# Block attention's scores issued for two heads at a time, alternating between two PSUM banks, in a one-core decoder block

## The chip, the cores and the metric

The kernel runs on one core of a Trainium2 chip. The metric is the device time of one execution in microseconds (us), the median over runs. TensorE is called PE in the views (its weight loads PEld), VectorE DVE, ScalarE ACT, GpSimd POOL, and SP issues the DMAs.

## The reference, cut to what matters

One hybrid decoder block for 256 tokens of 1024 features: three mixers in parallel (block attention "MoBA", retention, attention to a memory), a gated merge, and a convolutional GeGLU FFN. The change touches only the scores of the block attention, which has 8 heads of 64 features. With 256 tokens and a block of 256, only the query's own block remains, causally masked:

```python
s_own = (jnp.einsum('bhqd,bhnd->bhqn', q_c, k_own).astype(jnp.float32) * scale
         + table[:, rel_bucket(d_own)])
s_own = jnp.where(d_own >= 0, s_own, NEG_INF)
...
p = jax.nn.softmax(logits, axis=-1).astype(v.dtype)
...
return (jnp.einsum('bhqkn,bhqkne->bhqe', p_sel, v_sel)
        + jnp.einsum('bhqn,bhne->bhqe', p_own, v_own))
```

## The kernel before

Activations lie transposed, features on the 128 partitions and tokens on the free axis. The weights stream through in 150 pieces of [128, 1024]. Each piece is split into a high and a low part (ACT writes `whi` at L141, DVE writes `wlo` at L142), and each float32 product is carried by three passes of float32r matmuls: L183 in `unit` (256 columns each, 24 to a piece) and L170 to L172 in `proj_b` (512 columns). `piece()` issues the split three pieces ahead (`LA = 3`).

All small work is put between the pieces: `at(p, fn, ...)` registers it, and `tick()` runs it behind the matmuls of piece p. Every engine executes in the order of this program, so the place in it decides what is queued behind what.

For the block attention `qa` and `ka` are tiles of [128, 4, 256]: a feature tile f holds two heads, the even head on partitions 0 to 63 and the odd one on 64 to 127. `moba_s(h)` computes the scores of one head: one matmul for the later 128 queries against all 256 keys (L366) and one for the earlier 128 against the first 128 keys (L367, the rest is masked), both into one PSUM bank from `s_ps()` (two banks, `sps`). They are plain float32 matmuls with 64 rows, and the profile shows two weight loads and two matmuls for each. DVE then adds the bias (L369) into a scratch tile and takes two maxima (L372). `moba_e` (ACT, L379) exponentiates, `moba_n` (DVE, L385 and L387) normalises, `moba_t` transposes on PE (L391 to L393, read back by ACT at L394), and `moba_v` multiplies with the values for both heads of a feature tile (L405). Feature tile f starts at piece b = 16 + 3f:

```python
for f in range(4):
    b = 16 + 3 * f
    at(b + 5, moba_v, f)
    ...
    for hh in range(2):
        at(b + hh + 3, moba_t, 2 * f + hh)
        at(b + hh + 2, moba_n, 2 * f + hh)
        at(b + hh + 1, moba_e, 2 * f + hh)
        at(b + hh, moba_s, 2 * f + hh)
```

So the scores of the even head stand behind piece b and those of the odd head behind piece b + 1, with a piece of projection between them. Pieces 16 to 27 are the memory attention's projections; while they run, DVE and ACT also write the normed memory (L215 and L214, behind pieces 16 to 19).

`moba_v` is of use for comparison: its four matmuls go in turns to the output partitions 0 to 63 (even head) and 64 to 127 (odd head).

Of the kernel before, what the change touches and what calls it, by code (L numbers as in the profile page):

```python
"""Hybrid decoder block (MoBA attention + retention + memory cross-attention, gated merge, causal
conv GeGLU FFN) on one NeuronCore.

Layout: activations are kept transposed, [features on partitions, tokens on the free axis], so that
projections chain without transposes; values, the retention gate and the FFN output are
token-major.  Every float32 weight product is carried by float32r passes: an operand is split
exactly into hi (its top 12 significant bits) and lo (the rest), and hi*hi + hi*lo + lo*hi are
accumulated in float32.  With SEQ == MOBA_BLOCK no block lies fully in the past of any query, so
MoBA's selected blocks are masked for every query by the shapes alone and the causal own block
remains; likewise retention's state before the first chunk is zero.  # L10

Order: the weights stream through in pieces of [128, 1024] in the order of their use, and every
engine keeps the order of this program; the steps of the norms and of the mixers are set between the
pieces of later projections (at), so that TensorE always has work and no engine waits for the next.
"""
# [16 lines left out]
P = 128  # L32
D = 1024
# [6 lines left out]

# columns of the packed parameters
G_MEM, G_FFN, CONV_W, CONV_B = 0, 8, 16, 16 + 3 * 2 * NF
NPAR = CONV_B + 2 * NF
# columns of the packed constants
C_ID, C_COS, C_SIN, C_DEC, C_QIN, C_KOUT = 0, 128, 384, 640, 1152, 1664
NCONST = 1668
NREL = 384
NQ = 150      # pieces of the weights
LA = 3        # pieces split ahead of their use
WARM = 16  # L50
PASSES = ((0, 0), (0, 1), (1, 0))   # hi*hi + hi*lo + lo*hi
DEFER = 4     # FFN feature tiles that start from the h not yet normed
LAST = 3      # pieces of w_down that finish one group of outputs after the other


@with_exitstack
def block_kernel(ctx, tc, w, xt, mt, par, cst, onehot, relb, gng, gfin, out):
# [11 lines left out]

# [1 line left out]
    def mm_ps():  # L71
# [40 lines left out]

# [1 line left out]
    works = defaultdict(list)  # L114

    def at(p, fn, *args):
        """Run fn behind piece p."""
        works[p].append((fn, args))
# [4 lines left out]

# [1 line left out]
    raws, pieces = [], []  # L125
    count = {"used": 0}

    def load_ahead(n):
        """Start the loads of the first n pairs of pieces."""
        while len(raws) < min(n, NQ // 2):  # L130
            raws.append(raw8())
            nc.sync.dma_start(raws[-1], w[len(raws) - 1])
# [11 lines left out]
    def piece():  # L144
        """The next [128, 1024] piece of the weights as (hi, lo), with LA more split behind it."""
        while len(pieces) < min(NQ, count["used"] + 1 + LA):
            q = len(pieces)
            load_ahead(q // 2 + 3)
            piece_tiles()
            split_cols(q, 0, 1024)  # L150
        count["used"] += 1
        return pieces[count["used"] - 1]

    def split_to(dst, s, src):
        """dst[:, hi and lo, s] = src."""
        nc.scalar.copy(dst[:, 0, s], src)
        nc.vector.tensor_tensor(out=dst[:, 1, s], in0=src, in1=dst[:, 0, s].bitcast(FT), op=OP.subtract)

# [1 line left out]
    def proj_b(src, evac):  # L160
        """512 features, tokens on partitions."""
        ps = [mm_ps(), mm_ps()]
# [14 lines left out]
    def unit(p, hi, lo, o, step, src, nk):  # L177
        """One feature tile; the lo of the last two k, which comes last, is used last."""
        order = [(k, a, b) for k in range(nk - 2) for a, b in PASSES]
        order += [(k, a, 0) for k in (nk - 2, nk - 1) for a in (0, 1)] + [(k, 0, 1) for k in (nk - 2, nk - 1)]  # L180
        for i, (k, a, b) in enumerate(order):
            wk = (hi, lo)[a][:, o + step * k:o + step * k + P]
            nc.tensor.matmul(p, wk, src[:, b, k], start=(i == 0), stop=(i == len(order) - 1))  # L183

    def proj_a(src, banks=1):
        """256 features, features on partitions: a [128, 256] of a bank each."""
        ps = [mm_ps() for b in range(banks)]
        for f in range(2):
            hi, lo = piece()
            unit(ps[f % banks][:, T * f:T * f + T], hi, lo, 0, P, src, KD)  # L190
            tick()
        return kt(ps[0]) if banks == 1 else [kt(p)[:, f] for f, p in enumerate(ps)]

# [1 line left out]
    def rsqrt(dst, ss, n, scale):  # L195
# [4 lines left out]
    def squares(src, acc, i, scalar):  # L200
        """acc += x^2 of the features of pair i."""
        v = src[:, 2 * i:2 * i + 2]
# [14 lines left out]
    class Norm:  # L217
        """rsqrt(mean + eps) of each token, and src * gain * that, split."""

# [6 lines left out]
        def factor_col(self):  # L226
            """Tokens on partitions."""
            ps = t_ps()
# [4 lines left out]
        def factor_row(self):  # L233
            """As a row on all partitions."""
            ps = t_ps()
# [22 lines left out]

# [1 line left out]
    xs = big8()  # L260
# [27 lines left out]

# [1 line left out]
    mhalf = consts.tile([P, 2], FT, name="mhalf")  # L290
# [9 lines left out]

# [1 line left out]
    xg = act16()  # L302
# [15 lines left out]

# [1 line left out]
    nm = Norm("nm", mr, pr[:, G_MEM:G_MEM + KD], kt(w2()))  # L320
# [3 lines left out]

# [1 line left out]
    hank = mix.tile([P, 8, 384], FT, name="hank")  # L326
# [20 lines left out]

# [1 line left out]
    qa, ka, va = qk_tile(), qk_tile(), v_tile()  # L349
# [12 lines left out]

    def moba_s(h):
        f, pp = h // 2, slice(64 * (h % 2), 64 * (h % 2) + 64)
        sp = s_ps()
        nc.tensor.matmul(sp[:, 0:256], qa[pp, f, 128:256], ka[pp, f, :], start=True, stop=True)  # L366
        nc.tensor.matmul(sp[:, 256:384], qa[pp, f, 0:128], ka[pp, f, 0:128], start=True, stop=True)  # L367
        sb = w2()
        nc.vector.scalar_tensor_tensor(sb[:, :384], sp[:, :384], asc, hank[:, h, ::-1], op0=OP.mult, op1=OP.add)  # L369
        mx = act.tile([P, 2], FT, name="amx", bufs=2)  # L370
        for t, s in halves:
            nc.vector.tensor_reduce(out=mx[:, t:t + 1], in_=sb[:, s], axis=AX.X, op=OP.max, negate=True)  # L372
        mo["p", h] = sb, mx

# [36 lines left out]
    for f in range(4):  # L411
        b = 16 + 3 * f
        at(b + 5, moba_v, f)
        if f % 2 == 1:
            at(b + 6, moba_y, f // 2)
        for hh in range(2):
            at(b + hh + 3, moba_t, 2 * f + hh)
            at(b + hh + 2, moba_n, 2 * f + hh)
            at(b + hh + 1, moba_e, 2 * f + hh)
            at(b + hh, moba_s, 2 * f + hh)  # L420

# [1 line left out]
    qm, km = yt_tile(), yt_tile()  # L423
# [67 lines left out]

# [1 line left out]
    cos, sin = ct[:, C_COS:C_COS + T], ct[:, C_SIN:C_SIN + T]  # L493
# [19 lines left out]
    def ret_k():  # L513
        """Decay of chunk 0's keys to its end, times the factor of their norm (which v lacks)."""
        re["k"] = act.tile([P, 4], FT, name="rk", bufs=1)
        nc.vector.tensor_scalar(re["k"], ct[:, C_KOUT:C_KOUT + 4], nx.col[:, 0:1], None, op0=OP.mult)

    def ret_x():
        """Scores of chunk 1's queries with chunk 0's keys."""
        sp, sd = s_ps(), w2()  # L520
# [65 lines left out]

# [1 line left out]
    x2 = {}  # L588
# [35 lines left out]

# [1 line left out]
    hg = act16()  # L626
# [24 lines left out]

# [1 line left out]
    U0 = 84  # L653
# [44 lines left out]

# [1 line left out]
    groups = [[(0, 512, t_ps()), (512, 1024, t_ps())],  # L700
# [36 lines left out]
    def mean(t, i):  # L737
        """(sum of the squares up to group i) / D + eps."""
        v = act.tile([P, 1], FT, name="osv", bufs=4)
# [34 lines left out]

# [1 line left out]
def _constants():  # L776
# [8 lines left out]
    c[half:, C_COS:C_COS + T] = cos  # L785
    # read by the half that it multiplies: out1 -= x2 sin, out2 += x1 sin
    c[:half, C_SIN:C_SIN + T] = sin
# [5 lines left out]
    for h in range(4):  # L793
        c[:, C_DEC + P * h:C_DEC + P * h + P] = np.where(d >= 0, np.exp(lg[h] * np.maximum(d, 0)), 0.0) * ks
        c[:, C_QIN + P * h:C_QIN + P * h + P] = np.exp(lg[h] * (i + 1.0))[None, :]
        c[:, C_KOUT + h] = np.exp(lg[h] * (P - 1.0 - i)) * ks
    # one-hot of the bucket of distance m - 127
    dist = np.arange(NREL) - 127
# [79 lines left out]
```

## Time and profile before

| | us |
|---|---|
| median of 3 runs | 474.81 |
| lowest and highest run | 474.66 and 476.47 |
| span of the profiled execution, first to last instruction | 474.1 |
| PE busy in that span | 464.7 (98%) |
| DVE busy | 349.5 (74%) |
| ACT busy | 259.0 (55%) |

For the profiled execution only its span is on record, and no time of its own beside it; the median of the runs is about 0.7 us above that span. Matmuls are pipelined: a row's duration reaches from issue to a modelled end, and rows overlap. What a matmul costs is therefore read from the distance between the starts of neighbours, not from its duration.

### The profile page before, as it was taken

The numbers are of one execution on the slowest core, as the hardware profiler recorded it, in microseconds if no ns is written. First come the engines' busy times: TensorE is split into PE (matmuls) and PEld (weight loads), VectorE is DVE, ScalarE is ACT, GpSimd is POOL, SyncE is SP. The second block draws the span as 40 slices with busy tenths as digits, with TensorE's granted clock in tenths as the row PEclk, the third lists the DMA queues.
The fourth block names the chain that finished last, engine by engine and source line by source line (L and its number), as shares of the span: only waits on it lengthen the run. The fifth ranks groups of instructions, "written<-read, shape, count | busy, mean of one in ns | idle before, by whom it ended". The sixth has DMA issues, their size and how long they took to land.

```text
span 474.1 us, 8508 instructions
## 1 busy us (share of the span) xinstructions
PE 464.7 (98%) x3470; PEld 439.0 (93%) x3470; DVE 349.5 (74%) x536; ACT 259.0 (55%) x412; POOL 61.9 (13%) x47
## 2 busy tenths in 40 slices
PE   8999999999999999999999999999999999999994
PEld 6799899879989999999999999999999999888883
DVE  5969798766985558676677888979879899744433
ACT  5747465554455543354445555667768676533323
POOL 3344520001320013312000006000000000000003
PEclk9999999999999999999999999999999999999998
DMA  8989634335254544354464575555554545555102
GB/s 249 402 342 291 266 122 150 145 138 178 91 196 160 178 178 147 121 178 178 178 191 166 182 274 211 203 195 196 202 179 162 199 177 179 184 182 197 59 1 88
DMA packets 16342, 86.75 MB, mean 183 GB/s; under 512 B 1672, under 2 KB 4272, under 8 KB 6832
## 3 DMA queue, kind: packets, MB, share of 16 engines
q1 hardware_dynamic: 16016, 85.70, 50.8%
q8 instruction: 27, 0.44, 0.4%
q10 hardware_dynamic: 288, 0.52, 0.3%
q14 instruction: 11, 0.09, 0.1%
HBM read 85.15 MB, written 1.06 MB: 182 GB/s over the span
## 4 chain that ended last, share of the span: by engine, by line
PE 95%; DMA 1%; DVE 1%; ACT 1%; POOL 0%; SPq 0%; issue 0%; POOLq 0%; ACTq 0%
PE mm L183 67%; PE mm L172 3%; PE mm L170 3%; PE mm L171 3%; PE tps L706 2%; PE tps L707 2%; PE tps L708 2%; PE sps L706 1%; PE sps L707 1%; PE sps L708 1%; DMA big<-in_xt 1%; PE sps L366 1%; PE yps L405 1%; PE sps L439 1%; DVE wlo L142 1%; PE yps L476 1%
## 5 line engine op out<-in xcount | busy, mean ns | idle before, releaser
L183 PE MATMUL mm<-act,whi 128*128 128x256 f32 x1600 | 292.2, 282 | 0.0
L183 PEld LDWEIGHTS mm<-act,whi 128*128 128x128 f32 x1600 | 248.0, 188 | 1.8 <-issue 1.0
L142 DVE TENSOR_TENSOR wlo<-raw,whi 128x1024 fp32r<-128x1024 f32 (+1 forms) x154 | 195.4, 1273 | 65.3 <-ACT whi L141 65.0
L141 ACT CAST whi<-raw 128x1024 fp32r<-128x1024 f32 (+1 forms) x154 | 157.8, 1027 | 124.9 <-PE mm L183 75.1
L183 PE MATMUL mm<-act,wlo 128*128 128x256 f32 x800 | 215.5, 280 | 0.0
L183 PEld LDWEIGHTS mm<-act,wlo 128*128 128x128 f32 x800 | 150.7, 188 | 0.0
L674 DVE SCALAR_TENSOR_TENSOR w<-mm,pr,w 128x255 f32<-128x255 f32 (+1 forms) x72 | 29.7, 476 | 10.3 <-ACT w L669 10.2
L183 PE MATMUL mm<-yt,whi 128*128 128x256 f32 x192 | 36.6, 282 | 0.0
L183 PEld LDWEIGHTS mm<-yt,whi 128*128 128x128 f32 x192 | 30.4, 188 | 0.0
L170 PE MATMUL mm<-whi,act 128*128 128x512 f32 x64 | 26.7, 418 | 0.6 <-ACT whi L141 0.6
L669 ACT ACTIVATE w<-mm,pr 128x256 f32<-128x256 f32 x36 | 18.4, 561 | 16.3 <-PE mm L183 16.2
L172 PE MATMUL mm<-wlo,act 128*128 128x512 f32 x64 | 26.2, 410 | 1.0 <-DVE wlo L142 1.0
L171 PE MATMUL mm<-whi,act 128*128 128x512 f32 x64 | 26.1, 408 | 0.0
L183 PE MATMUL mm<-yt,wlo 128*128 128x256 f32 x96 | 25.1, 282 | 0.0
L735 POOL TENSOR_TENSOR hN<-hN,gfb 128x512 f32<-128x512 f32 x2 | 2.6, 1281 | 169.8 <-ACT w L731 169.8
L183 PEld LDWEIGHTS mm<-yt,wlo 128*128 128x128 f32 x96 | 18.1, 188 | 0.0
L505 POOL TENSOR_TENSOR qk<-qk,w 128x512 f32<-128x512 f32 x4 | 9.3, 2314 | 65.7 <-DVE w L503 65.7
L706 PE MATMUL tps<-whi,ah 128*128 128x512 f32 x44 | 17.5, 397 | 0.0
L707 PE MATMUL tps<-whi,ah 128*128 128x512 f32 x44 | 17.4, 396 | 0.0
L172 PEld LDWEIGHTS mm<-wlo,act 128*128 128x128 f32 x64 | 12.4, 194 | 5.4 <-DVE wlo L142 2.5
L708 PE MATMUL tps<-wlo,ah 128*128 128x512 f32 x44 | 17.3, 393 | 0.0
L170 PEld LDWEIGHTS mm<-whi,act 128*128 128x128 f32 x64 | 12.5, 195 | 3.9 <-ACT whi L141 0.9
(162 smaller groups left out, 512.8 us busy)
## 6 DMA issues: line engine op xcount, KB each, us to landing
raw<-in_w SPq DMA_DIRECT2D x72, 1024.0 KB, 4.8
raw<-in_w SPq DMA_DIRECT2D x8, 256.0 KB, 5.8
raw<-in_w SPq DMA_DIRECT2D x2, 512.0 KB, 6.3
big<-in_mt SPq DMA_DIRECT2D x1, 1024.0 KB
hank<-rel_d SPq DMA_DIRECT2D x1, 1024.0 KB, 11.8
raw<-in_xt SPq DMA_DIRECT2D x1, 1024.0 KB, 5.0
ct<-in_cst SPq DMA_DIRECT2D x1, 770.0 KB, 4.4
big<-in_xt SPq DMA_DIRECT2D x3, 256.0 KB, 6.0
```

Source lines behind the costliest of these rows:

```text
L141: nc.scalar.copy(hi[:, a:b], r)
L142: nc.vector.tensor_tensor(out=lo[:, a:b], in0=r, in1=hi[:, a:b].bitcast(FT), op=OP.subtract)
L170: nc.tensor.matmul(ps[t], xh, wh, start=(k == 0), stop=False)
L171: nc.tensor.matmul(ps[t], xl, wh, start=False, stop=False)
L172: nc.tensor.matmul(ps[t], xh, wl, start=False, stop=(k == KD - 1))
L183: nc.tensor.matmul(p, wk, src[:, b, k], start=(i == 0), stop=(i == len(order) - 1))
L505: nc.gpsimd.tensor_tensor(out=d, in0=d, in1=tmp, op=OP.add)
L669: nc.scalar.activation(ac[:, i], ps[:, i], AF.Identity, bias=pr[:, CONV_B + c:CONV_B + c + 1], scale=cw(2, c))
L674: nc.vector.scalar_tensor_tensor(ac[:, i, s:], ps[:, i, :T - s], cw(2 - s, c), ac[:, i, s:], op0=OP.mult, op1=OP.add)
L706: nc.tensor.matmul(p, xh, hi[:, a:b], start=(f == 0), stop=False)
L707: nc.tensor.matmul(p, xl, hi[:, a:b], start=False, stop=False)
L708: nc.tensor.matmul(p, xh, lo[:, a:b], start=False, stop=(f == NF - 1))
```

## The change

`moba_s` now takes a feature tile instead of a head. It takes both PSUM banks, issues the 256-key matmuls of the even and the odd head, then the 128-key matmuls of both, and then does the DVE work of the even head and of the odd head. It runs behind piece b; nothing is left behind piece b + 1. The other steps keep their pieces. (The change also empties docstrings and comments, which moves no instruction and no line number ahead of `moba_s`; behind it lines move by 4.)

```diff
-    def moba_s(h):
-        f, pp = h // 2, slice(64 * (h % 2), 64 * (h % 2) + 64)
-        sp = s_ps()
-        nc.tensor.matmul(sp[:, 0:256], qa[pp, f, 128:256], ka[pp, f, :], start=True, stop=True)
-        nc.tensor.matmul(sp[:, 256:384], qa[pp, f, 0:128], ka[pp, f, 0:128], start=True, stop=True)
-        sb = w2()
-        nc.vector.scalar_tensor_tensor(sb[:, :384], sp[:, :384], asc, hank[:, h, ::-1], op0=OP.mult, op1=OP.add)
-        mx = act.tile([P, 2], FT, name="amx", bufs=2)
-        for t, s in halves:
-            nc.vector.tensor_reduce(out=mx[:, t:t + 1], in_=sb[:, s], axis=AX.X, op=OP.max, negate=True)
-        mo["p", h] = sb, mx
+    def moba_s(f):
+        sps = [s_ps(), s_ps()]
+        for q, k, o in ((slice(128, 256), 256, 0), (slice(0, 128), 128, 256)):
+            for hh in range(2):
+                pp = slice(64 * hh, 64 * hh + 64)
+                nc.tensor.matmul(sps[hh][:, o:o + k], qa[pp, f, q], ka[pp, f, :k], start=True, stop=True)
+        for hh in range(2):
+            h, sp, sb = 2 * f + hh, sps[hh], w2()
+            nc.vector.scalar_tensor_tensor(sb[:, :384], sp[:, :384], asc, hank[:, h, ::-1], op0=OP.mult, op1=OP.add)
+            mx = act.tile([P, 2], FT, name="amx", bufs=2)
+            for t, s in halves:
+                nc.vector.tensor_reduce(out=mx[:, t:t + 1], in_=sb[:, s], axis=AX.X, op=OP.max, negate=True)
+            mo["p", h] = sb, mx
...
     for f in range(4):
...
+        at(b, moba_s, f)
         for hh in range(2):
             at(b + hh + 3, moba_t, 2 * f + hh)
             at(b + hh + 2, moba_n, 2 * f + hh)
             at(b + hh + 1, moba_e, 2 * f + hh)
-            at(b + hh, moba_s, 2 * f + hh)
```

What PE has behind piece 16 before, between that piece (weights `whi_580`) and piece 17 (`whi_602`): the scores of head 0 alone, in one bank (`sps_688`).

```order
L183 MATMUL mm_654<-act16_436,whi_580 128x256 x2
L366 MATMUL sps_688<-qk_264,qk_263 128x256
L367 MATMUL sps_688<-qk_264,qk_263 128x128
L183 MATMUL mm_654<-act16_436,whi_602 128x256 x2
L366 MATMUL sps_733<-qk_264,qk_263 128x256
```

(The last row, head 1, stands behind piece 17, 23 more matmuls of L183 later.) And at the same place with the change, `sps_688` for head 0 and `sps_689` for head 1:

```order
L183 MATMUL mm_654<-act16_436,whi_580 128x256 x2
L370 MATMUL sps_688<-qk_264,qk_263 128x256
L370 MATMUL sps_689<-qk_264,qk_263 128x256
L370 MATMUL sps_688<-qk_264,qk_263 128x128
L370 MATMUL sps_689<-qk_264,qk_263 128x128
L183 MATMUL mm_654<-act16_436,whi_602 128x256 x2
```

The two matmuls of head 1 have moved up by one piece, in between those of head 0; behind piece 17 nothing stands between the projections.

What DVE has from the memory's norm of piece 16 (`w_622`) to the split of the first memory queries (L157, `yt`), as a difference; `w_691` and `w_694` are the scratch tile of head 0, `w_699` that of head 1:

```order
 L215 SCALAR_TENSOR_TENSOR act_683<-w_622,pr,act_683 128x256 x2
-L369 SCALAR_TENSOR_TENSOR w_691<-sps,hank 128x384
-L372 TENSOR_REDUCE amx<-w_691 128x1 x2
+L373 SCALAR_TENSOR_TENSOR w_694<-sps,hank 128x384
+L376 TENSOR_REDUCE amx<-w_694 128x1 x2
+L373 SCALAR_TENSOR_TENSOR w_699<-sps,hank 128x384
+L376 TENSOR_REDUCE amx<-w_699 128x1 x2
 L142 TENSOR_TENSOR wlo<-raw,whi 128x1024
 L215 SCALAR_TENSOR_TENSOR act_683<-w_624,pr,act_683 128x256 x2
-L369 SCALAR_TENSOR_TENSOR w_736<-sps,hank 128x384
-L372 TENSOR_REDUCE amx<-w_736 128x1 x2
 L157 TENSOR_TENSOR yt<-mm,yt 128x512
```

Head 1's bias and maxima have moved ahead of one split of weights (L142) and one pair of the memory's norm; what stands ahead of L157 is the same work in sum.

What PE has behind piece 19 before, where the transposes of head 0 (L391 to L393, which read its normalised scratch tile) stand ahead of head 2's scores:

```order
L183 MATMUL mm_743<-act16_436,whi_655 128x256 x2
L391 MATMUL tps_817<-ct_93,w2_691 128x128
L392 MATMUL tps_817<-ct_93,w2_691 128x128
L393 MATMUL tps_817<-ct_93,w2_691 128x128
L366 MATMUL sps_827<-qk_264,qk_263 128x256
L367 MATMUL sps_827<-qk_264,qk_263 128x128
L183 MATMUL mm_837<-act16_683,whi_698 128x256 x2
```

With the change the transposes stay where they were, and the scores of heads 2 and 3 follow them:

```order
L183 MATMUL mm_743<-act16_436,whi_655 128x256 x2
L395 MATMUL tps_817<-ct_93,w2_694 128x128
L396 MATMUL tps_817<-ct_93,w2_694 128x128
L397 MATMUL tps_817<-ct_93,w2_694 128x128
L370 MATMUL sps_827<-qk_264,qk_263 128x256
L370 MATMUL sps_828<-qk_264,qk_263 128x256
L370 MATMUL sps_827<-qk_264,qk_263 128x128
L370 MATMUL sps_828<-qk_264,qk_263 128x128
L183 MATMUL mm_845<-act16_683,whi_706 128x256 x2
```

Only the scores have moved here: PE reaches these transposes with one block of scores less behind it than before.

## Rows read from the trace of the kernel before

**Rows 1.** The page, part 1: busy us (share of the span) xinstructions.

```profile
PE 464.7 (98%) x3470; PEld 439.0 (93%) x3470; DVE 349.5 (74%) x536; ACT 259.0 (55%) x412; POOL 61.9 (13%) x47
```

**Rows 2.** The page, part 4: the chain that ended last, by engine.

```profile
PE 95%; DMA 1%; DVE 1%; ACT 1%; POOL 0%; SPq 0%; issue 0%; POOLq 0%; ACTq 0%
```

**Rows 3.** Stretches A:B: length, busy us of PE, PEld, DVE, ACT, POOL, clock, DMA share, GB/s.

```profile
57.00:101.00 44.00, 44.00 (x298) 38.45 (x297) 33.43 (x66) 26.34 (x61) 4.85 (x3) 1.00 0.37 129
300.00:400.00 100.00, 100.00 (x852) 100.00 (x851) 88.50 (x159) 70.15 (x119) 0.00 (x0) 1.00 0.53 182
```

**Rows 4.** Groups by form, PE: busy us, mean ns | idle before.

```profile
L366 PE MATMUL sps<-qk 64*128 64x256 f32 x16 | 5.6, 428 | 0.0
```

**Rows 5.** Timeline, PE, head 0's scores behind piece 16: start us, us, instruction.

```profile
59.65 0.28 PE L183 MATMUL mm<-act,whi 128*128 128x256 f32 x1
59.87 0.48 PE L366 MATMUL sps<-qk 64*128 64x256 f32 x1
60.19 0.38 PE L366 MATMUL sps<-qk 64*128 64x256 f32 x1
60.40 0.27 PE L367 MATMUL sps<-qk 64*128 64x128 f32 x1
60.51 0.27 PE L367 MATMUL sps<-qk 64*128 64x128 f32 x1
60.71 0.50 PE L183 MATMUL mm<-act,whi 128*128 128x256 f32 x2
61.05 0.28 PE L183 MATMUL mm<-act,wlo 128*128 128x256 f32 x1
```

**Rows 6.** The chain in order of time: an undisturbed run of L183.

```profile
158.52 14.25 PE mm L183 x120
```

**Rows 7.** Timeline, PE, the value products of heads 0 and 1 behind piece 21.

```profile
78.69 0.28 PE L183 MATMUL mm<-act,whi 128*128 128x256 f32 x1
78.89 0.44 PE L405 MATMUL yps<-w,vv 128*64 128x256 f32 x2
79.16 0.50 PE L405 MATMUL yps<-w,vv 128*64 128x256 f32 x4
79.38 0.39 PE L405 MATMUL yps<-w,vv 128*64 128x128 f32 x4
79.70 0.51 PE L183 MATMUL mm<-act,whi 128*128 128x256 f32 x2
80.04 0.28 PE L183 MATMUL mm<-act,wlo 128*128 128x256 f32 x1
```

**Rows 8.** Timeline, PE: transposes with L183 directly behind them, behind piece 28.

```profile
107.18 0.27 PE L393 MATMUL tps<-ct,w 128*128 128x128 f32 x1
107.21 0.48 PE L183 MATMUL mm<-act,whi 128*128 128x256 f32 x2
```

**Rows 9.** Timeline, DVE: bias of heads 0 and 1, one weight split, the normalisations.

```profile
62.45 0.54 DVE L369 SCALAR_TENSOR_TENSOR w<-sps,hank 128x384 f32<-128x384 f32 x1
...
63.56 1.22 DVE L142 TENSOR_TENSOR wlo<-raw,whi 128x1024 fp32r<-128x1024 f32 x1
...
65.48 0.56 DVE L369 SCALAR_TENSOR_TENSOR w<-sps,hank 128x384 f32<-128x384 f32 x1
...
69.32 0.55 DVE L387 TENSOR_SCALAR w<-w,ari 128x256 f32<-128x256 f32 x2
...
71.91 0.55 DVE L387 TENSOR_SCALAR w<-w,ari 128x256 f32<-128x256 f32 x2
```

**Rows 10.** The stretch of DVE from behind piece 16's norm to head 0's normalisation.

```profile
60.62:69.87 9.25, 9.25 (x74) 8.85 (x73) 9.15 (x20) 7.17 (x18) 1.23 (x1) 1.00 0.37 120
```

**Rows 11.** Timeline, PE: first transposes of heads 0 and 1, first wlo of piece 20.

```profile
70.37 0.27 PE L391 MATMUL tps<-ct,w 128*128 128x128 f32 x1
...
71.98 0.28 PE L183 MATMUL mm<-act,wlo 128*128 128x256 f32 x1
...
74.59 0.27 PE L391 MATMUL tps<-ct,w 128*128 128x128 f32 x1
```

## The prediction

> **What bounds the kernel now.** I read the page first, then the stretches, then PE's timeline round the scores. PE is busy for 464.7 of 474.1 us [rows 1], and 95% of the chain that ended last is PE's [rows 2]. In the stretch that holds all scores, 57 to 101 us, PE is busy for all of its 44.00 us, and it is so again from 300 to 400 us, where DVE comes nearest to it with 88.5 of 100 us [rows 3]. The granted clock is 1.00 in both, the upper level of 2.4 GHz. So the place of the change is bounded by PE's own stream, and what the scores take from that stream is time of the kernel, as long as nobody else becomes late. The views show starts of matmuls; I use only distances between starts.
>
> **What one block of scores costs.** Undisturbed L183 runs at 14.25 / 120 = 0.119 us per matmul [rows 6]. From the last L183 of piece 16 at 59.65 to the third L183 of piece 17 at 61.05 is 1.40 us [rows 5]. Without scores that is three steps, 0.36. Head 0's block therefore costs **1.04 us**, and 8 heads 8.3 us. The starts inside say what it consists of. The two passes of 128 columns start 0.11 apart (60.40 and 60.51), and the second pass of 256 columns takes 0.21 (60.19 to 60.40): columns alone make 2 x 0.21 + 2 x 0.11 = 0.64. The other 0.40 is paid once for each block: 0.09 more than a normal step before the first pass (59.65 to 59.87), 0.11 more for the first pass (0.32 instead of 0.21, as its successor's weights are not loaded in time), 0.09 more behind the last pass (60.51 to 60.71 is 0.20, its columns 0.11), and 0.10 more behind the first L183, whose two starts lie 0.50 - 0.28 = 0.22 apart. All 16 instructions of this form [rows 4] are 8 heads' two passes, one such block each.
>
> **What the change does to it.** Before, 8 blocks of 2 matmuls (4 passes) each; after, 4 blocks of 4 matmuls (8 passes). No column is saved. Four times the 0.40 of entering and leaving is saved in any case. Whether the columns of the odd head cost anything is not shown by any block of scores, because no two matmuls on different row halves are neighbours in this trace. The bounds are: full cost, 0.64 per pair, or nothing, if the two halves of the array stream at the same time.
>
> The nearest row is L405, which alternates between two column halves of the array in the same pattern: even head, odd head, even, odd, with 256 columns twice and then 128 columns twice. Its 8 passes start as four couples at 78.89, 79.16, 79.38 and one between that and 79.70; the row at 78.89 holds two passes in 0.44 us, less than the 0.48 of the first score pass alone [rows 5, 7]. From 78.69 to 80.04 the whole takes 1.35, less 0.36 for three L183 steps: **0.99 us for two heads**, although the columns of its 8 passes, at the prices above, are 4 x 0.21 + 4 x 0.11 = 1.28 us. So two half arrays do stream at the same time there. I take the same for two row halves: a pair of heads then costs what one head costs now, 1.04. Nothing in the rows is nearer, and it is the same engine, the same float32 passes and the same order of issue.
>
> By the Trainium skill, "TensorE: Matmul & The Clock Gate", Part 3 (packing small matmuls), matmuls whose operands lie on different row groups run concurrently, with a measured 3.07x for four of them. The same page of the Trainium skill says that matmuls keep strict program order, which speaks against full couples (a rival below). The trace agrees with the concurrency on column halves; no run here shows it for row halves. The Trainium skill, "TensorEngine Tiling (Array Packing)", Gotcha 1, states that different row tiles cannot access one PSUM bank at the same time; the change gives each head a bank, and no run here shows two in one.
>
> **The sum before waits.** Four blocks vanish, behind pieces 17, 20, 23 and 26. The block behind piece 17 stands between two runs of L183 and saves 1.04. The other three stand behind transposes. There L183 would start 0.03 behind L393, and the second of it 0.48 - 0.28 = 0.20 later [rows 8], so nearly the same is left over: I take 4 x 1.04 = **4.18 us** with the unrounded block of 1.045.
>
> **What becomes late.** PE will be 1.04 us earlier when it comes to the transposes of head 0 behind piece 19: 70.37 - 1.04 = 69.33 [rows 11]. They read the tile that DVE normalises at L387, which ends at 69.32 + 0.55 = 69.87 [rows 9]. Can DVE be earlier too? From 60.62 to 69.87 it is busy for 9.15 of 9.25 us [rows 10]: it is working off a backlog, in which head 0's bias starts at 62.45, 1.7 us behind the scores. The change only reorders this backlog (head 1's bias and maxima, about 1.2 us from 65.48, move ahead of the split at 63.56), so the end stays at 69.87. PE then waits 0.54 us, and the first transpose's weights, no longer loaded ahead, cost another 0.1, as behind each block above. I take **0.65 us given back**; bounds are 0 (DVE earlier by as much) and 1.04 (the whole advance).
>
> Queued behind that wait are the scores of heads 2 and 3, which DVE takes at the end of the same backlog, and piece 20. The next such place is safe: head 1's tile is done at 71.91 + 0.55 = 72.46 [rows 9], and PE comes for it at 74.59 - 1.04 + 0.65 = 74.2 [rows 11]. For heads 2 to 7 the road from scores to transposes gets one block, about 1 us, shorter on PE, but DVE's backlog is gone there: over 57 to 101 us it is busy for only 33.43 of 44 us [rows 3].
>
> The rest costs nothing. The weight split at 63.56 ends 1.2 us later, at 66.0, and PE uses its first low part at 71.98 [rows 9, 11], or 0.4 earlier with the change: 5.6 us cover it; without cover the whole 1.2 would fall on PE. Both banks are asked for together, but their readers of the tile before are DVE steps three pieces (over 9 us) back. No DMA is issued at another place; behind 101 us everything simply comes earlier, and PE is fed without a gap [rows 3].
>
> Net: 4.18 - 0.65 = 3.53 us. The span should go from 474.1 to 470.6, and with the same 0.7 us around it the time from 474.81 to **471.3 us**, -0.74%. With no wait it is 470.6; with the weight loads of the two halves taking turns (0.11 more for each of four pairs) 471.7. That is the forecast's own range, 470.5 to 471.7. About 0.5% (2.4 us) is what a measurement of this kernel can tell from no change.
>
> **Rivals.**
>
> *Strict order.* The odd head may start only when both passes ahead of it have started: then its first pass runs beside the even head's second, and one pass of 256 columns per pair stays uncovered, 0.21 us. The gain is 4 x 0.83 = 3.3; PE comes to head 0's transposes at 69.54 and gives back 0.45. Net 2.9, time **471.9**. For it: the odd head's matmul is issued behind both passes of the even one. Against it: L405 has that same order of issue and starts in couples [rows 7]. This rival is the rule of the Trainium skill named above ("TensorE: Matmul & The Clock Gate", Part 3, matmuls in strict order); the trace disagrees with it on column halves.
>
> *Row halves don't stream together.* Only the four times 0.40 remain, 1.6 us; PE comes at 69.97, so no wait. Time **473.2**, which measures as no change: the edit wouldn't do what it is made for. For it: a row half writes all 128 output partitions, so two of them write twice as much per partition as L405 does. Against it: each has a bank of its own.
>
> *Each turn drains the array.* Entering or leaving a 64-row block costs 0.09 of gap and 0.11 of uncovered load [rows 5]. If a turn from one row half to the other did the same, 3 turns in each of 4 pairs add 12 x 0.20 = 2.4 us to a serial pair: 2.4 - 1.6 = 0.8 slower, **475.6**. It is slower than before from 0.13 us per turn, and slower by over 0.5% from (1.6 + 2.4) / 12 = 0.33. For it: a change of shape costs just that. Against it: L405's turns cost nothing visible.
>
> **How the numbers follow.** Forecast 0.68, strict order 0.10, no overlap 0.14, drains 0.05, something unseen 0.03. The likeliest gives 471.3. Forecast and strict order together hold 0.78, just under what a range should, so it reaches to the third case: 470.4 to 473.3. Faster by over 0.5% are the first two (0.77 with a little off), within it the third and most of the fourth (0.18), slower the rest (0.05).
>
> **What would show it.** Right: four blocks of scores instead of eight; in each the 8 passes start as four couples, and from the L183 ahead of them to the third behind them it is again about 1.40 us; behind piece 17 L183 runs on at 0.119; one wait of PE, about half a microsecond, at the transposes behind piece 19, put down to DVE's L391; and PE ahead by about 3.5 us from there to the end. Wrong: eight separate starts in a block (1.4 + 0.64 us long), gaps of 0.2 us between the heads' passes, or PE waits at later transposes or at a low part of the weights, which would say that DVE or ACT could not follow.

## The result and the profile after

The changed kernel takes **471.81 us** (median of 4 runs, 471.54 to 472.01), against 474.99 for the kernel before (4 runs, 474.66 to 476.47). The ratio is **0.9932, interval 0.992 to 0.9944**: faster by 3.2 us, with an interval of 2.7 to 3.8. The forecast was 471.3 us, a gain of 3.5 us and a ratio of 0.9926.

The page after, part 1, beside [rows 1]:

```profile
PE 460.1 (98%) x3470; PEld 435.7 (93%) x3470; DVE 348.7 (74%) x536; ACT 258.1 (55%) x412; POOL 61.8 (13%) x47
```

The instructions are the same in number; PE has 4.6 us less busy time. The block behind piece 16, on PE's timeline of the kernel after, beside [rows 5] (start us, us, instruction; a row with x2 or x4 merges so many passes, named by the first one's shape):

```profile
58.72 0.28 PE L183 MATMUL mm<-act,whi 128*128 128x256 f32 x1
58.93 0.49 PE L370 MATMUL sps<-qk 64*128 64x256 f32 x2
...
59.25 0.49 PE L370 MATMUL sps<-qk 64*128 64x256 f32 x4
...
59.58 0.28 PE L370 MATMUL sps<-qk 64*128 64x128 f32 x2
59.78 0.50 PE L183 MATMUL mm<-act,whi 128*128 128x256 f32 x2
60.12 0.28 PE L183 MATMUL mm<-act,wlo 128*128 128x256 f32 x1
```

Two passes of 256 columns start at 58.93 and run together: both are over in 0.49 us, and one alone took 0.48 in [rows 5]. The row at 59.25 holds the next two couples, and the last couple stands at 59.58. From the L183 ahead (58.72) to the third behind (60.12) it is 1.40 us: the length that one head had in [rows 5], now for two.

What came in addition is the wait that was forecast, at the transposes of head 0 behind piece 19, beside [rows 11]. PE's timeline there, with the idle time and its releaser at the end of the row:

```profile
68.10 0.40 PE L183 MATMUL mm<-act,whi 128*128 128x256 f32 x2
69.08 0.30 PE L395 MATMUL tps<-ct,w 128*128 128x128 f32 x1 [0.58 <-DVE w L391]
```

The last L183 started at 68.10 + 0.40 - 0.28 = 68.22. The next start would normally be 0.12 later, but it comes 0.86 later: **0.74 us**. DVE's timeline of the same kernel shows why, beside [rows 9]:

```profile
61.52 0.55 DVE L373 SCALAR_TENSOR_TENSOR w<-sps,hank 128x384 f32<-128x384 f32 x1
...
62.62 0.55 DVE L373 SCALAR_TENSOR_TENSOR w<-sps,hank 128x384 f32<-128x384 f32 x1
...
68.38 0.55 DVE L391 TENSOR_SCALAR w<-w,ari 128x256 f32<-128x256 f32 x2
```

Both heads' bias steps stand together now, and head 0's normalisation still ends 6.86 + 0.55 us behind the first of them, as it did before (62.45 to 69.87, 7.42). The tile is done at 68.38 + 0.55 = 68.93, and PE would have come at 68.34: 0.59 of the 0.74 us is waiting for the tile, and 0.15 lies between its end and the first transpose.

All of PE's waits that the profile lists, before and then after (who waited for whom: us in total, times, longest):

```profile
PE tps L299 <- DVE zero L295: 1.2, 1, 1.2
PE mm L172 <- DVE wlo L142: 1.0, 3, 0.7
PE mm L170 <- ACT whi L141: 0.6, 1, 0.6
```

```profile
PE tps L299 <- DVE zero L295: 1.2, 1, 1.2
PE mm L170 <- ACT whi L141: 0.7, 1, 0.7
PE tps L395 <- DVE w L391: 0.6, 1, 0.6
PE mm L172 <- DVE wlo L142: 0.5, 2, 0.3
```

The row of L395 is the new one; it is the only one of these that lies behind the first score.

The 4.3 us between the two spans (474.1 and 469.8) are not the effect of the change alone. The first score starts at 59.87 in [rows 5] and at 58.93 here, 0.94 earlier, and nothing that was changed lies ahead of it. The profiled execution of the kernel before was a long one: 20 later executions of it have spans of 472.7 to 473.6. A fair measure is the time from the first score to the last matmul. Its end on PE's timeline, first of the kernel before, then of the one after:

```profile
467.36 0.28 PE L708 MATMUL sps<-wlo,ah 128*128 128x256 f32 x1
```

```profile
462.97 0.28 PE L712 MATMUL sps<-wlo,ah 128*128 128x256 f32 x1
```

Before: 467.36 - 59.87 = 407.49. After: 462.97 - 58.93 = 404.04. The difference is **3.45 us**, and 3.45 + 0.74 = 4.19 without the wait. The prediction had 3.53 and 4.18.

### The profile page after: what moved, and what is told of

The parts are those of the page before. It is cut to its first block, busy times and chain, and to the rows that moved or that the text cites. A ratio compares the mean times of both kernels' runs of the same rounds, so it can differ in the third digit from the quotient of the medians.

```text
span 469.8 us, 8509 instructions
## 1 busy us (share of the span) xinstructions
PE 460.1 (98%) x3470; PEld 435.7 (93%) x3470; DVE 348.7 (74%) x536; ACT 258.1 (55%) x412; POOL 61.8 (13%) x47
## 4 chain that ended last, share of the span: by engine, by line
PE 91%; DVE 3%; DMA 1%; issue 1%; SPq 1%; ACT 1%; POOL 0%; POOLq 0%; ACTq 0%; DVEq 0%
PE mm L183 65%; PE mm L172 3%; PE mm L170 3%; PE mm L171 3%; PE tps L710 2%; PE tps L711 2%; PE tps L712 2%; PE sps L710 1%; PE sps L711 1%; PE sps L712 1%; DVE wlo L142 1%; DMA raw<-in_w 1%; DVE act L215 1%; PE yps L409 1%; PE sps L443 1%
## 5 line engine op out<-in xcount | busy, mean ns | idle before, releaser
L183 PE MATMUL mm<-act,whi 128*128 128x256 f32 x1600 | 291.7, 282 | 0.0
L183 PEld LDWEIGHTS mm<-act,whi 128*128 128x128 f32 x1600 | 247.9, 188 | 1.5 <-issue 1.0
L142 DVE TENSOR_TENSOR wlo<-raw,whi 128x1024 fp32r<-128x1024 f32 (+1 forms) x154 | 196.2, 1278 | 65.9 <-ACT whi L141 65.7
L183 PE MATMUL mm<-act,wlo 128*128 128x256 f32 x800 | 215.4, 280 | 0.0
L183 PEld LDWEIGHTS mm<-act,wlo 128*128 128x128 f32 x800 | 150.6, 188 | 0.0
L183 PE MATMUL mm<-yt,whi 128*128 128x256 f32 x192 | 36.6, 282 | 0.0
L183 PEld LDWEIGHTS mm<-yt,whi 128*128 128x128 f32 x192 | 30.4, 188 | 0.0
L183 PE MATMUL mm<-yt,wlo 128*128 128x256 f32 x96 | 25.1, 282 | 0.0
L183 PEld LDWEIGHTS mm<-yt,wlo 128*128 128x128 f32 x96 | 18.1, 188 | 0.0
```

Of the source, the lines that this page charges most:

```text
L142: nc.vector.tensor_tensor(out=lo[:, a:b], in0=r, in1=hi[:, a:b].bitcast(FT), op=OP.subtract)
```

## The experiments

The theory: two row halves of the array stream at the same time, a pair of heads costs what one head cost, and 0.7 us of the gain goes into a wait for DVE's backlog. The rivals: only the number of blocks matters; passes start in strict order; the wait has another cause, or its time is lost anyway. All kernels below are the changed one with one edit, timed against the kernel before.

**Are row halves the point?** Both heads' matmuls read the same half of the partitions, so the odd heads' scores are those of the even heads.

```diff
-                pp = slice(64 * hh, 64 * hh + 64)
+                pp = slice(0, 64)
```

> The change with one edit: both heads read partitions 0 to 63, so all 8 passes of a block are on one row half (the odd head's scores are then those of the even head, a different computation). If the gain rests on two row halves streaming at once, no couples are left: a block takes 1.40 + 0.64 = 2.04 us, 4 x 0.64 = 2.56 us are lost, 0.6 come back as a shorter wait behind piece 19, and 1.3 to 1.6 us (four entries and exits of 0.40) are all that is left of the gain: ratio 0.9966 to 0.9973. If the gain comes only from having four blocks instead of eight, nothing changes against the change: 0.993.

Measured: 473.26 us, ratio 0.9971 (0.996 to 0.9981). PE's timeline of this kernel, the block behind piece 16:

```profile
58.24 0.28 PE L183 MATMUL mm<-act,whi 128*128 128x256 f32 x1
58.45 0.48 PE L370 MATMUL sps<-qk 64*128 64x256 f32 x1
...
58.77 0.59 PE L370 MATMUL sps<-qk 64*128 64x256 f32 x2
...
59.21 0.48 PE L370 MATMUL sps<-qk 64*128 64x256 f32 x2
...
59.53 0.49 PE L370 MATMUL sps<-qk 64*128 64x128 f32 x3
...
59.75 0.27 PE L370 MATMUL sps<-qk 64*128 64x128 f32 x1
59.96 0.50 PE L183 MATMUL mm<-act,whi 128*128 128x256 f32 x2
60.30 0.28 PE L183 MATMUL mm<-act,wlo 128*128 128x256 f32 x1
```

The first pass starts alone at 58.45, the second 0.32 later, and so on, eight starts one by one (the row at 59.53 holds the last three, the last of them at 59.75). From 58.24 to 60.30 it is 2.06 us instead of 1.40: 0.66 more, where the prediction had 0.64 of columns per pair. From the first score to the last matmul it is 464.40 - 58.45 = 405.95, 1.54 us less than before. So about 1.5 us of the 4.2 come from entering and leaving blocks of 64-row matmuls four times less, and the rest from the two halves streaming together.

**Does the order of issue matter?** The same matmuls, head by head instead of in turns:

```diff
-        for q, k, o in ((slice(128, 256), 256, 0), (slice(0, 128), 128, 256)):
-            for hh in range(2):
+        for hh in range(2):
+            for q, k, o in ((slice(128, 256), 256, 0), (slice(0, 128), 128, 256)):
```

> The change with one edit: the two heads' score matmuls stand behind the same piece, but head by head (even 256, even 128, odd 256, odd 128 columns) instead of in turns. If the array may start a pass of the other row half although passes of the first half are queued ahead of it, the 8 passes again start as four couples, a block takes 1.40 us as in the change, and the ratio to the kernel before stays near 0.993. If passes start in strict order, the odd head's first pass starts only beside the even head's last (128 columns): the block takes 1.40 + 0.64 - 0.11 = 1.93 us, 4 x 0.53 = 2.1 us are lost, of which 0.53 come back as a shorter wait behind piece 19; about 1.6 us slower than the change, ratio near 0.9966.

Measured: 471.56 us, ratio 0.993 (0.9918 to 0.9943). PE's timeline of this kernel, the same block:

```profile
58.86 0.28 PE L183 MATMUL mm<-act,whi 128*128 128x256 f32 x1
59.07 0.49 PE L370 MATMUL sps<-qk 64*128 64x256 f32 x2
...
59.39 0.50 PE L370 MATMUL sps<-qk 64*128 64x256 f32 x4
...
59.93 0.50 PE L183 MATMUL mm<-act,whi 128*128 128x256 f32 x2
60.27 0.28 PE L183 MATMUL mm<-act,wlo 128*128 128x256 f32 x1
```

Two passes of 256 columns start at 59.07, although four passes of the even head are now issued ahead of the first of the odd one; the block takes 1.41 us. Strict order falls: the odd head's first pass didn't wait for the four ahead of it. (The sentence further up that every engine executes in the order of the program is therefore too wide: the starts of these passes on PE don't keep it.) "In turns" is therefore not what makes the change work; standing behind the same piece, on different row halves, is.

**Is the wait real time, and is it DVE's backlog?** First the waiting transposes were moved back by one piece, behind piece 20:

```diff
-            at(b + hh + 3, moba_t, 2 * f + hh)
+            at(b + hh + 3 + (f == 0 and hh == 0), moba_t, 2 * f + hh)
```

> The change with one edit: the transposes of head 0 stand behind piece 20 instead of 19, ahead of those of head 1. If PE's wait behind piece 19 (a step of 0.86 us instead of 0.12) is real time of the kernel, it goes and nothing takes its place, since head 0's tile is then long done and head 1's is done 0.8 us before PE comes: 0.7 us faster than the change, ratio near 0.9917. If the time is lost anyway (PE then waits at head 1's transposes or at a split of the weights), the ratio stays near 0.993.

Measured: 470.64 us, ratio 0.991 (0.9897 to 0.9924). Then only DVE's order was changed, head 0's normalisation ahead of the memory norm's pair behind piece 18:

```diff
-            at(b + hh + 2, moba_n, 2 * f + hh)
+            if f == 0 and hh == 0:
+                works[b + 2].insert(0, (moba_n, (0,)))
+            else:
+                at(b + hh + 2, moba_n, 2 * f + hh)
```

> The change with one edit: behind piece 18 DVE normalises head 0 ahead of the memory norm's pair (two steps of 0.4 us) instead of behind it. If the wait behind piece 19 comes from DVE's backlog, head 0's tile is done 0.8 us earlier, about 0.1 to 0.2 us before PE comes, and the wait of 0.7 us goes: ratio near 0.9917, and the memory norm, done 0.5 us later, is still in time for piece 20. If something else holds PE there, nothing changes: 0.993.

Measured: 470.60 us, ratio 0.9914 (0.9901 to 0.9928). DVE's timeline of this last kernel, and then PE's:

```profile
67.30 0.55 DVE L391 TENSOR_SCALAR w<-w,ari 128x256 f32<-128x256 f32 x2
67.77 0.87 DVE L215 SCALAR_TENSOR_TENSOR act<-w,pr,act 128x256 fp32r<-128x256 f32 x2
```

```profile
67.81 0.40 PE L183 MATMUL mm<-act,whi 128*128 128x256 f32 x2
68.05 0.27 PE L395 MATMUL tps<-ct,w 128*128 128x128 f32 x1
```

Head 0's tile is done at 67.85, PE comes to it at 68.05 without a gap, and the memory norm's pair (L215) simply follows. From the first score to the last matmul it is 461.89 - 58.65 = 403.24 here and 461.98 - 58.70 = 403.28 with the later transposes, 4.2 us less than before in both: the whole 4.18 of the sum before waits. So the wait is time of the kernel, and it is the work that DVE has queued ahead of this tile that makes it. In the runs, the two come out 1.0 to 1.2 us below the change, and 0.9 to 1.0 below the head-by-head kernel that was timed beside them, where the profiles have 0.8; the intervals are too wide to tell these apart.

**Does it matter where DVE does the odd head's work?** PE as in the change, but the odd head's bias and maxima behind piece b + 1 as before:

```diff
-        for hh in range(2):
-            h, sp, sb = 2 * f + hh, sps[hh], w2()
+        mo["s", f] = sps
+
+    def moba_b(h):
+        sp, sb = mo["s", h // 2][h % 2], w2()
...
         at(b, moba_s, f)
+        at(b, moba_b, 2 * f)
...
+            if hh:
+                at(b + 1, moba_b, 2 * f + 1)
```

> The change with one edit: PE's scores of both heads stay together, but DVE's bias and maxima of the odd head stand behind piece b + 1, as before the change. If the moved DVE work costs nothing and the wait behind piece 19 is set by the sum of DVE's backlog, not by its order, then head 0's tile is done at the same place in it, PE waits there as in the change, and the time is that of the change: ratio near 0.993, within 0.001. If the odd head's DVE work, moved up, is what makes head 0's tile late, the wait of 0.7 us goes: ratio near 0.9917. If moving it up is worth something, this kernel is slower than the change.

Measured: 471.39 us, ratio 0.9928 (0.9914 to 0.9941), the time of the change. PE's timeline has the same wait:

```profile
68.65 0.30 PE L397 MATMUL tps<-ct,w 128*128 128x128 f32 x1 [0.58 <-DVE w L393]
```

So moving the DVE work cost nothing here, and the wait is set by the sum of what DVE has ahead of the normalisation, not by the order within it.

**The change again**, as it is:

> The changed kernel as it is, timed beside the others: ratio 0.993 with four blocks of about 1.40 us (from the L183 ahead to the third behind) and one wait of 0.6 us at the transposes behind piece 19. No theory differs here; it says how far two profiles of one kernel differ in the first 20 us, ahead of the place of the change.

Measured: 471.61 us, ratio 0.9932 (0.992 to 0.9945), with the same block and the same wait. From the first score to the last matmul it is 463.20 - 59.16 = 404.04, as in the first profile of this kernel. Ahead of the change the two differ by 0.23 us (58.93 and 59.16).

Not tried: two row halves into one PSUM bank. A head's scores take 384 of the 512 columns of an `sps` tile, so two heads don't fit into one, and no run here has two row halves writing one bank at once. Whether a bank of its own is needed beyond the room stays open.

## Why the prediction was right

- *PE's stream bounds the place.* Right: what vanished from the stream came off the time, less the wait below.
- *One block costs 1.04 us, 0.64 of it columns.* Right: with the overlap taken away a block is 0.66 longer (2.06 against 1.40).
- *Two row halves stream at once, read from column halves in [rows 7].* Right: four couples, 1.40 us for two heads. The extrapolation was the open point of the forecast, and the same-half kernel shows that it carries more than half of the gain (1.54 us without it, 3.45 with it). The bound that weight loads of the two halves might take turns (0.11 per pair) did not come up.
- *Four blocks saved, 4.18 us.* Right in size: 4.19 in the profile, and 4.2 in both kernels without the wait. (From the rows as shown, a block is 1.40 - 3 x 0.119 = 1.043 rather than 1.045, and the sum 4.17.)
- *0.65 us given back behind piece 19.* Right in place and cause, a little small: 0.74, made of 0.59 of waiting for the tile (forecast 0.54) and 0.15 from its end to the first transpose (forecast 0.1, put down to the weight load). The normalisation ended as long behind the first bias step as before; the two kernels that take away the wait, one on PE's side and one on DVE's, give its time back.
- *Nothing else late.* Right: it is the only wait of PE that the change adds; head 1's transposes and all later ones are reached without one.
- *Time.* 3.2 us by medians (2.7 to 3.8) against 3.5; the profiles, from the first score on, have 3.45. The median is 0.5 above the forecast, just outside the 470.5 to 471.7 that the prediction calls the forecast's own range, and nearer to the 471.9 of strict order. The time alone doesn't tell these two apart; the couples in the block and the head-by-head kernel do. Nor does the wide range (470.4 to 473.3) say much for the mechanism, as it takes in no overlap too. About 0.2 of the 0.5 is the median of before, which was 474.81 in the runs shown ahead of the prediction and 474.99 with one more run; the rest is inside the interval.
- *The same 0.7 us around the span.* Not so: in every execution with both figures on record, the time is 1.7 to 1.9 us above the span. The 0.7 came from the long profiled execution of the kernel before. The time forecast doesn't depend on it (474.81 - 3.53); the span forecast does (470.6, measured 469.8).

*Strict order* falls with the head-by-head kernel. *No overlap* (473.2) is what the same-half kernel, which leaves out the second half, comes to: 473.26. *A drain at each turn* falls: the passes of a couple start about 0.01 us apart (0.49 us for two, 0.48 for one), and the block is no longer than that of one head.

The best version is the change with head 0's normalisation, or its transposes, moved by one place: 470.6 us, ratio 0.991.

## What to carry to other kernels

Matmuls that use half of the array's rows are worth collecting where PE's stream bounds the time: put those of the two halves behind each other, each into a bank of its own as here. In this kernel the second half's columns then cost nothing (1.40 us for one head and for two). Entering and leaving such a block has a price (0.40 us here), so fewer and longer blocks paid even without overlap (1.54 us). And when PE is made faster at one place, look up what it comes to next: the tile that was done half a microsecond early before is the next wait, and here one move in the late engine's order took it away.

## What had not been expected of the hardware

The order of issue within a block made no difference. With four passes of the even head issued first, the odd head's first pass still started together with the even head's first, as the head-by-head profile shows (two passes of 256 columns from 59.07 on, ratio 0.993 as in the change). The Trainium skill, "TensorE: Matmul & The Clock Gate", Part 3, says that matmuls start and end strictly in program order. For passes on different row halves the starts of this trace disagree; the ends in it are modelled and say nothing on this.

The first 20 us differ between profiles by more than the wait that was studied here: the first L183 starts at 20.78 in the kernel before and at 19.97 in the kernel after, on instructions that are the same in both. The seven profiles of the kernels with the change lie between 19.50 and 20.17. What makes the difference isn't shown. Spans of two single profiles are therefore compared from the place of the change on.
